# A decoder layer's MLP with its activation tiles 32 bytes lower in SBUF

## The chip, the cores and the metric

The kernel runs on one core of a Trainium2 chip. The metric is the device time of one execution in microseconds (us); 1 us is 1000 ns. A "matmul" below is one matmul instruction of TensorE: it streams a **moving** operand (up to 512 columns, one result column each) past a **stationary** operand (128 columns), which a weight load (LDWEIGHTS, engine name PEld in the profile) has put into the array before.

## The reference

One layer of a hybrid decoder on 512 tokens of width 1024, in float32. The change lies in the last part, the MLP:

```python
h = h + mixed @ w_o[l]
a = jax.nn.relu(rmsnorm(h, g_mlp_norm[l]) @ w_up[l])   # (512, 4096)
h = h + (a * a) @ w_down[l]                            # (512, 1024)
...
return rmsnorm(h, g_final)
```

## The kernel before

**Split products.** Every float32 operand is split into a high and a low part (`split`, L121), and a product is three matmuls, `mm3` (L129): high times high, high times low, low times high, into one PSUM bank. In the profile L130, L131 and L132 are these three.

**The MLP.** The 4096 hidden columns are done in four quarters (L1132). A quarter first computes two units of up-projection (`up_unit`, L1005; the first of all is `up_plain`, L1044), 512 hidden columns each, and then two halves of down-projection (L1141), 512 output columns each. The up-projection's matmuls (L991) have 256 columns: the stationary operand is a 128-column slice of a weight tile `uw`, the moving operand 256 columns of a token tile `tt...`. The down-projection's matmuls (`down`, L1148) have 512 columns: the stationary operand is a 128-column slice of the activations, `ah` (high part) or `al` (low part), and the moving operand is half a row of a tile `dw` of W_down. In the last half of the last quarter the fourth token block is done in pieces of 256 columns (`pieces`, L1127). TensorE does its matmuls in program order; the loads, splits and additions for later tiles run on the other engines beside them.

**Where the tiles lie.** A tile's address is the same in all 128 partitions, and pools are laid behind each other in the order in which they are opened:

- The pool `nsa` holds the five slots (`slot`, L934) in which the weight tiles `uw` and `dw` lie. A slot has 2048 or 2176 columns of 4 bytes: 16 or 17 times 512 bytes. The pool's other tiles are multiples of 512 bytes too.
- Then comes the pool `mh` (L925): a tile `shift` of 8 columns (32 bytes) that nothing reads, then the seven tiles `tt` of 8192 bytes, and raw weights and sums of 4096 bytes each.
- Then comes the pool `mlp` (L1094): a tile `back` of 120 columns (480 bytes) that nothing reads, then `gf` (4096 bytes, the final gain), seven tiles `c` of 2048 bytes (snapshots, `re`, `v`, `jh`, `jf`, `fin`), and eight tiles `ah` and eight `al` of 2048 bytes.

All slices that the matmuls take start at multiples of 128 columns, which is 512 bytes. So, counted in multiples of 512 bytes, `ah` and `al` lie at the same place as `uw` and `dw` (32 + 480 = 512), and `tt` lies 32 bytes above it.

Of the kernel before, what the change touches and what calls it, by code (L numbers as in the profile page):

```python
# [10 lines left out]
F32 = mybir.dt.float32  # L11
# [6 lines left out]
P = 128  # L18
# [76 lines left out]
def layer(ctx, tc, x, xt, w_in, w_uq, w_ukv, w1k, w2k, w1v, w2v, w_o, w_up, w_down, g_final, consts, vecs, out):  # L95
# [997 lines left out]
    m["wo"].release()  # L1093
    mp = ctx.enter_context(tc.tile_pool(name="mlp", **reuse))  # L1094

    mp.tile([P, 120], F32, name="back")
    gf = mp.tile([P, D], F32, name="gf")
    sync.dma_start(gf, g_final.unsqueeze(0).to_broadcast([P, D]))
    fs, rf, fin = col(80, 16), col(40), {}
# [162 lines left out]
```

## Time and profile before

| | |
|---|---|
| median of 3 runs | 648.17 us (647.2 to 648.53) |
| the profiled execution | 648.08 us |
| its span, first to last instruction | 646.2 us |
| TensorE matmuls busy | 628.8 us (97%) |
| mean granted TensorE clock | 0.999 |

The span is what the rows show; the 1.9 us between it and the execution's time lie around it. Start times in the rows count from the start of the span. A matmul's own duration contains its way through the array; what the next one has to wait is the step from one start to the next, which is read from the start times.

### The profile page before, as it was taken

What the parts mean: (1) busy time and instruction counts of PE and PEld (TensorE: products, weight loads), DVE (VectorE), ACT (ScalarE), POOL (GpSimd) and SP (SyncE); (2) the same over time, 40 slices, a digit from 0 to 9 for tenths busy, and PEclk for the clock granted to TensorE, in tenths of its full rate; (3) what the DMA queues carried; (4) which work ended last, traced back from release to release, by engine and by line L of the source; (5) the groups of instructions that cost most, each with busy time, mean ns of one, the idle gap of its engine ahead of it and who ended that gap; (6) DMA issues with size and microseconds to landing.
All of it is one profiled execution on the core that took longest, in us unless ns stands there. A gap on an engine that the chain in (4) does not pass through costs nothing.

```text
span 646.2 us, 10981 instructions
## 1 busy us (share of the span) xinstructions
PE 628.8 (97%) x4092; PEld 568.1 (88%) x4092; DVE 430.4 (67%) x898; ACT 337.2 (52%) x702; POOL 243.2 (38%) x294
## 2 busy tenths in 40 slices
PE   7989999999999999999999999999999999999996
PEld 5989999998878888888998889988899888999885
DVE  5767577756778598869967436784259843497425
ACT  5567677867946487741794115451144521355213
POOL 3764402235783138713111325413155231354031
PEclk9999999999999999999999999999999999999999
DMA  6533210105323101063035313254121542124003
GB/s 192 161 92 87 69 43 25 33 2 183 97 83 101 32 2 34 2 194 133 33 101 166 126 33 99 70 183 139 33 73 63 183 139 67 64 68 146 17 2 130
DMA packets 47125, 56.53 MB, mean 87 GB/s; under 512 B 4320, under 2 KB 34784, under 8 KB 47072
## 3 DMA queue, kind: packets, MB, share of 16 engines
q1 hardware_dynamic: 46784, 55.57, 27.5%
q8 instruction: 32, 0.52, 0.3%
q10 hardware_dynamic: 288, 0.26, 0.1%
q14 instruction: 21, 0.17, 0.1%
HBM read 53.72 MB, written 2.10 MB: 86 GB/s over the span
## 4 chain that ended last, share of the span: by engine, by line
PE 86%; DVE 5%; DMA 3%; ACT 2%; POOL 2%; issue 1%; SPq 1%; POOLq 0%; ACTq 0%; DVEq 0%
PE up_ps L991 25%; PE dn_ps L131 9%; PE dn_ps L132 9%; PE dn_ps L130 9%; PE wo_ps L132 2%; PE wo_ps L130 2%; PE wo_ps L131 2%; PE pt_ps L585 2%; PE hid_ps L730 2%; PE pt_ps L692 1%; PE s_ps L547 1%; PE ot_ps L596 1%; PE wq_ps L131 1%; PE wq_ps L132 1%; PE wq_ps L130 1%
## 5 line engine op out<-in xcount | busy, mean ns | idle before, releaser
L130 PE MATMUL dn_ps<-dw,ah 128*128 128x512 f32 (+1 forms) x264 | 101.1, 383 | 0.0
L131 PE MATMUL dn_ps<-dw,ah 128*128 128x512 f32 (+1 forms) x264 | 101.1, 383 | 0.0
L132 PE MATMUL dn_ps<-dw,al 128*128 128x512 f32 (+1 forms) x264 | 100.8, 383 | 0.0
L991 PE MATMUL up_ps<-ttT,uw 128*128 128x256 f32 x720 | 87.8, 279 | 1.9 <-ACT snap L1020 1.9
L991 PEld LDWEIGHTS up_ps<-ttT,uw 128*128 128x128 f32 x720 | 85.6, 188 | 2.5 <-ACT snap L1020 2.5
L991 PE MATMUL up_ps<-ttB,uw 128*128 128x256 f32 x648 | 80.4, 279 | 0.0
L991 PEld LDWEIGHTS up_ps<-ttB,uw 128*128 128x128 f32 x648 | 78.1, 188 | 0.5
L959 POOL TENSOR_TENSOR us<-us,ur 128x1024 f32<-128x1024 f32 x14 | 41.7, 2978 | 96.3 <-DVE uw L125 96.3
L959 POOL TENSOR_TENSOR us<-ur 128x1024 f32<-128x1024 f32 x14 | 35.0, 2511 | 98.3 <-DMA ur<-in_w_up 49.2
L125 DVE TENSOR_TENSOR dw<-dr,dw 128x1024 fp32r<-128x1024 f32 x32 | 44.0, 1374 | 33.5 <-ACT dw L111 33.5
L125 DVE TENSOR_TENSOR uw<-us,uw 128x1024 fp32r<-128x1024 f32 x28 | 34.2, 1223 | 45.6 <-ACT uw L111 45.6
L131 PEld LDWEIGHTS dn_ps<-dw,ah 128*128 128x128 f32 x264 | 49.6, 188 | 9.7
L130 PEld LDWEIGHTS dn_ps<-dw,ah 128*128 128x128 f32 x264 | 49.6, 188 | 9.7
L132 PEld LDWEIGHTS dn_ps<-dw,al 128*128 128x128 f32 x264 | 49.5, 188 | 9.6
L111 ACT CAST uw<-us 128x1024 fp32r<-128x1024 f32 x28 | 29.4, 1051 | 54.3 <-PE dn_ps L132 39.7
L125 DVE TENSOR_TENSOR uw<-ur,uw 128x1024 fp32r<-128x1024 f32 x25 | 40.1, 1605 | 25.0 <-ACT uw L111 25.0
L111 ACT CAST dw<-dr 128x1024 fp32r<-128x1024 f32 x32 | 33.3, 1050 | 36.2 <-PE dn_ps L132 20.8
L111 ACT CAST uw<-ur 128x1024 fp32r<-128x1024 f32 x25 | 26.3, 1051 | 28.7 <-PE dn_ps L132 26.2
L125 DVE TENSOR_TENSOR pl<-pt_ps,ph 128x512 fp32r<-128x512 f32 (+3 forms) x60 | 34.3, 578 | 8.2 <-ACT ph L111 7.0
L560 ACT ACTIVATE pr<-pr,mx 128x256 f32<-128x256 f32 (+3 forms) x64 | 36.0, 565 | 6.5 <-DVE mx L552 4.6
L111 ACT CAST ph<-pt_ps 128x512 fp32r<-128x512 f32 (+3 forms) x60 | 29.7, 499 | 15.6 <-PE pt_ps L585 5.4
L1158 DVE SCALAR_TENSOR_TENSOR xs<-dn_ps,small,xs 128x512 f32<-128x512 f32 (+1 forms) x33 | 22.8, 734 | 19.0 <-PE dn_ps L132 19.0
(326 smaller groups left out, 1540.5 us busy)
## 6 DMA issues: line engine op xcount, KB each, us to landing
ur<-in_w_up SPq DMA_DIRECT2D x32, 512.0 KB, 3.8
dr<-in_w_down SPq DMA_DIRECT2D x32, 512.0 KB, 3.7
wor<-in_w_o SPq DMA_DIRECT2D x16, 256.0 KB, 3.0
wqraw<-in_w_in SPq DMA_DIRECT2D x16, 128.0 KB, 2.2
xs<-in_x SPq DMA_DIRECT2D x4, 512.0 KB, 5.1
wmraw<-in_w_in SPq DMA_DIRECT2D x8, 208.0 KB, 4.5
xr<-in_xt SPq DMA_DIRECT2D x3, 512.0 KB, 3.6
out<-xs SPq DMA_DIRECT2D x6, 256.0 KB, 2.2
```

What stands on the lines that cost most here:

```text
L111: nc.scalar.copy(dst, src)
L125: (lo_eng or nc.vector).tensor_tensor(lo, src, hi.bitcast(F32), op=ALU.subtract)
L130: nc.tensor.matmul(o, a_hi, b_hi, start=first, stop=False)
L131: nc.tensor.matmul(o, a_hi, b_lo, start=False, stop=False)
L132: nc.tensor.matmul(o, a_lo, b_hi, start=False, stop=last)
L547: nc.tensor.matmul(S[:, :b - a], qs, ka[:, brg, a:b], start=True, stop=False)
L560: nc.scalar.activation(pr[:, :L], pr[:, :L], AF.Exp, bias=lim, scale=-1.0, accum_out=sums[:, 4 + h:5 + h])
L585: nc.tensor.transpose(b[:, h * P:(h + 1) * P], prs[h][:, j * P:(j + 1) * P], ident)
L730: nc.tensor.matmul(hp[0:96, 0:P], xx[:, 2 * i:2 * i + 16 * 95 + 1:16], w1[:, j, :], start=(i == 0), stop=(i == 15))
L959: add = lambda o, x, y: nc.gpsimd.tensor_tensor(o, x, y, op=ALU.add)
L991: nc.tensor.matmul(oj, v[:, x, k, s], t[:, y, k, :], start=first and j == 0 and k == 0 and n == 0, stop=k == 3 and n == 2, skip_group_chec ...
L1158: nc.vector.scalar_tensor_tensor(xs[:, t, cs], accs[t, a][:, a:b], r4[:, t:t + 1], xs[:, t, cs], op0=ALU.mult, op1=ALU.add)
```

## The change

The unread tile `back` shrinks from 120 to 112 columns, from 480 to 448 bytes. Everything in the pool `mlp`, `gf`, `c`, `ah` and `al`, then lies 32 bytes lower. No instruction is added, removed or moved to another place in its queue. `uw`, `dw` and `tt` stay where they are. Counted in multiples of 512 bytes, `dw` then lies 32 bytes above `ah` and `al`.

```diff
-    mp.tile([P, 120], F32, name="back")
+    mp.tile([P, 112], F32, name="back")
     gf = mp.tile([P, D], F32, name="gf")
```

## Rows read from the trace of the kernel before

**Rows 1.** The profile page: span, busy time of TensorE, granted TensorE clock in tenths over 40 slices, and the shares of the chain that ended last.

```profile
span 646.2 us, 10981 instructions
...
PE 628.8 (97%) x4092; PEld 568.1 (88%) x4092; DVE 430.4 (67%) x898; ACT 337.2 (52%) x702; POOL 243.2 (38%) x294
...
PEclk9999999999999999999999999999999999999999
...
PE 86%; DVE 5%; DMA 3%; ACT 2%; POOL 2%; issue 1%; SPq 1%; POOLq 0%; ACTq 0%; DVEq 0%
```

**Rows 2.** Matmuls by line and shape from 344.7 to 640 us (four quarters but the first up-projection): count, busy us, mean ns of one, idle us before them.

```profile
L131 PE MATMUL dn_ps<-dw,ah 128*128 128x512 f32 x248 | 96.6, 389 | 0.0
L130 PE MATMUL dn_ps<-dw,ah 128*128 128x512 f32 x248 | 96.6, 389 | 0.0
L132 PE MATMUL dn_ps<-dw,al 128*128 128x512 f32 x248 | 96.5, 389 | 0.0
L991 PE MATMUL up_ps<-ttT,uw 128*128 128x256 f32 x577 | 70.8, 279 | 1.9 <-ACT snap L1020 1.9
L991 PE MATMUL up_ps<-ttB,uw 128*128 128x256 f32 x432 | 53.9, 279 | 0.0
L132 PE MATMUL dn_ps<-dw,al 128*128 128x256 f32 x16 | 4.5, 282 | 0.0
L131 PE MATMUL dn_ps<-dw,ah 128*128 128x256 f32 x16 | 4.5, 282 | 0.0
L130 PE MATMUL dn_ps<-dw,ah 128*128 128x256 f32 x16 | 4.5, 281 | 0.0
```

**Rows 3.** Busy time of each engine, with its count of instructions, the granted clock and the DMA share, in an up-projection unit (388 to 408 us) and in the two halves of the down-projection that follow the next one.

```profile
388.00:408.00 20.00, 20.00 (x173) 19.96 (x172) 13.75 (x12) 9.92 (x12) 11.90 (x5) 1.00 0.27 84
...
428.30:450.00 21.70, 21.70 (x98) 17.98 (x97) 12.71 (x16) 5.87 (x7) 5.00 (x2) 1.00 0.50 158
450.00:471.90 21.90, 21.90 (x99) 18.12 (x98) 7.83 (x9) 4.20 (x4) 4.79 (x2) 1.00 0.13 41
```

**Rows 4.** The second quarter's down-projection: its first matmul, the first one of the up-projection behind it, and (by line, 428.4 to 471.8 us) the count of one of its three lines.

```profile
428.32 0.39 PE L130 MATMUL dn_ps<-dw,ah 128*128 128x512 f32 x1
...
471.85 0.86 PE L991 MATMUL up_ps<-ttB,uw 128*128 128x256 f32 x6
...
L131 PE MATMUL dn_ps<-dw,ah 128*128 128x512 f32 x64 | 24.9, 389 | 0.0
```

**Rows 5.** The last pieces of the down-projection, 256 columns each: the first two and the last of 23 matmuls that follow each other without another instruction of TensorE between them.

```profile
636.89 0.28 PE L131 MATMUL dn_ps<-dw,ah 128*128 128x256 f32 x1
637.01 0.28 PE L132 MATMUL dn_ps<-dw,al 128*128 128x256 f32 x1
...
639.53 0.28 PE L132 MATMUL dn_ps<-dw,al 128*128 128x256 f32 x1
```

**Rows 6.** The instructions in order of time: start us, duration us. A matmul of the down-projection and the weight load for the next one.

```profile
615.90 0.39 PE L132 MATMUL dn_ps<-dw,al 128*128 128x512 f32 x1
615.91 0.19 PEld L130 LDWEIGHTS dn_ps<-dw,ah 128*128 128x128 f32 x1
```

**Rows 7.** The chain that ended last, in order of time: start us, length us, line and count of the matmuls. Three stretches of up-projection without a wait.

```profile
307.87 36.87 PE up_ps L991 x316
388.31 33.62 PE up_ps L991 x288
...
472.01 33.62 PE up_ps L991 x288
```

**Rows 8.** Two projections at the start of the kernel: the first and the last of 31 matmuls of `wm_ps` (416 columns) and of 24 matmuls of `wk_ps` (256 columns), each without another instruction of TensorE between them.

```profile
21.39 0.34 PE L130 MATMUL wm_ps<-wmh,xth 128*128 128x416 f32 x1
...
27.06 0.36 PE L130 MATMUL wm_ps<-wmh,xth 128*128 128x416 f32 x1
...
43.13 0.28 PE L130 MATMUL wk_ps<-wkh,xth 128*128 128x256 f32 x1
...
45.85 0.28 PE L132 MATMUL wk_ps<-wkh,xtl 128*128 128x256 f32 x1
```

**Rows 9.** ScalarE copies of 128 by 512 from PSUM, to a tile of the pool `mlp` and to tiles of two other pools: count, busy us, mean ns.

```profile
L1020 ACT COPY snap<-up_ps 128x512 f32<-128x512 f32 x21 | 12.3, 583 | 12.0 <-PE up_ps L991 12.0
L637 ACT COPY os<-ot_ps 128x512 f32<-128x512 f32 x16 | 9.3, 584 | 8.4 <-PE ot_ps L597 6.1 <-PE ot_ps L704 2.3
L590 ACT COPY pb<-pt_ps 128x512 f32<-128x512 f32 x12 | 7.0, 582 | 1.7 <-PE pt_ps L585 1.7
```

**Rows 10.** An up-projection behind a wait of 0.64 us: its last 45 matmuls in two merged rows; the down-projection begins at 428.32 us [rows 4].

```profile
422.91 3.10 PE L991 MATMUL up_ps<-ttT,uw 128*128 128x256 f32 x24 [0.64 <-ACT snap L1020]
425.84 2.63 PE L991 MATMUL up_ps<-ttB,uw 128*128 128x256 f32 x21
```

**Rows 11.** The first quarter's down-projection: its first matmul and the eleventh.

```profile
344.57 0.40 PE L130 MATMUL dn_ps<-dw,ah 128*128 128x512 f32 x1
...
346.89 0.39 PE L131 MATMUL dn_ps<-dw,ah 128*128 128x512 f32 x1
```

## The prediction, made before the changed kernel ran

> **What bounds the kernel now.** I read the page first. TensorE is busy for 97% of the span, at the upper of its two clock levels (2.4 GHz) in every slice, and holds 86% of the chain that ended last [rows 1]. So the time is the sum of TensorE's steps, and only what changes such a step, or opens a gap between two, can move it. Next I read the matmuls by line and shape: from 344.7 us on, the down-projection is 744 matmuls of 512 columns and 48 of 256, 792 in all, with no idle time before any of them; the only idle time is 1.9 us in the up-projection, waiting for a snapshot on ScalarE [rows 2]. The table of stretches shows how much room the others have: in the down-projection's two halves TensorE is busy throughout, while VectorE works 12.7 and 7.8 us of 21.8, ScalarE 5.9 and 4.2 [rows 3]. The reader is to see that nobody else sets the pace there.
>
> Last I read the steps from start to start, since the 389 ns that a row gives for a 512-column matmul contain its way through the array. The second quarter's down-projection takes 471.85 - 428.32 = 43.53 us for 3 x 64 = 192 matmuls: **226.7 ns** each [rows 4]. Its small pieces of 256 columns take (639.53 - 636.89) / 22 = **120.0 ns** [rows 5]. 256 more columns cost 106.7 ns, so a column costs 0.417 ns (one at each beat of 2.4 GHz), and both shapes carry the same extra: 226.7 - 213.3 = 120.0 - 106.7 = **13.3 ns** a matmul, whatever its length.
>
> **Where the 13.3 ns may come from.** The weight load for the next matmul starts 0.01 us behind the start of the present one and lasts 0.19 us [rows 6]: two streams read SBUF side by side, the moving operand and the next stationary one. If they get into each other's way, it matters how their addresses stand to each other, and it costs per weight load, not per column, as the 13.3 ns do. The kernel has the test built in. The up-projection has the same three-matmul pattern, 256 columns and 128 stationary columns, but its moving tile `tt` lies 32 bytes above the stationary `uw`, modulo 512. It steps by 36.87/316 = 116.7, 33.62/288 = 116.7 and again 116.7 ns [rows 7]. Same shape, other distance: 116.7 against 120.0. The extra is **10.0 ns** at 32 bytes against 13.3 at zero, 3.3 less. The means of one say the same, 279 against 282 ns [rows 2].
>
> Two other stages fit. The `wm` projection's tiles are 416 columns, 13 times 128 bytes, so its distances are multiples of 128 bytes; it steps by (27.06 - 21.39)/30 = 189.0 ns, and 416 columns at 0.417 are 173.3: an extra of 15.7. The `wk` projection's tiles are 280 columns (35 times 32 bytes), so its distance changes with every tile through all multiples of 32; it steps by (45.85 - 43.13)/23 = 118.3, an extra of 11.6, between the two [rows 8]. So a distance that stays at zero (modulo 128) is the dear end, a mixture lies between, and a steady 32 bytes is the cheap end of what the trace shows.
>
> **The change part by part.** (1) `ah` and `al` move down 32 bytes, `dw` stays: the moving operand then lies 32 bytes above the stationary one, with the sign and the size that the up-projection has now. The trace has no 512-column matmul at that distance. From the cheap side the nearest row is the up-projection's 10.0 ns [rows 7], from the dear side no gain, 13.3 [rows 4], or even `wm`'s 15.7 [rows 8]. I take 10.0: the extra did not depend on the length at distance zero, so I let it not depend on it at 32 bytes, and order and lines of the three matmuls are the same. The sum: 792 x 3.33 ns = **2.64 us** less. A 512-column step would be 223.3 ns, a half of the down-projection 96 x 223.3 = 21.44 us instead of 21.76.
>
> (2) `gf` and the `c` tiles move too. Their users are ScalarE, VectorE and GpSimd. ScalarE's 128 by 512 copy takes 583 ns into a `c` tile and 584 and 582 ns into tiles of two other pools that lie elsewhere [rows 9], so I cost the shift at nothing. What hides it is TensorE's unbroken stream [rows 2]; without that cover 2 ns on the 21 snapshots would be 0.04 us.
>
> (3) Is anything late when the down-projection is 0.32 us shorter per half? What must be ready by then are the next weight tiles. ScalarE and VectorE rest for at least 9 us in each half [rows 3], and no matmul there waits [rows 2]. The three waits of 0.64 us for a snapshot [rows 10] lie inside an up-projection and are timed from its own matmuls; they stay.
>
> The Trainium skill speaks against this change. Its page "TensorE: Matmul & The Clock Gate", section "Step-by-step: what each phase is for", gives TensorE two independent read ports of SBUF and says that loading the next weights takes no read bandwidth from the running matmul; its section "Back-to-back issue gap" puts the step at N/2.4 + 2.5 ns, an estimate of 109.2 ns for 256 columns. The trace disagrees: the same shape steps by 120.0 and 116.7 ns [rows 5, 7]. By that page the change would do nothing.
>
> **Rivals.**
>
> *Half the gain.* TensorE can settle into more than one rhythm at the same distance. Behind the wait, the up-projection's 21 matmuls take 428.32 - 425.84 = 2.48 us, 118.1 ns each [rows 4, 10], an extra of 11.4, and it stays so up to the down-projection. Today the rhythm re-forms there, as the distance changes; with equal distances it might be carried over. `wk`'s mixture has about the same extra, 11.6 [rows 8]. Gain (13.3 - 11.4) x 792 = 1.5 us: 646.6 us.
>
> *No change.* The 3.3 ns belong to something else that differs between the up- and the down-projection: where the moving operand itself lies (`tt` against `dw`, and `dw` does not move), or 512 columns hide what 256 do not. For it: in the rows of one stage the distance never varies alone. Against it: 13.3 at both lengths [rows 4, 5]. Time 648.1. This is also where the skill's two ports end.
>
> *Slower.* The two streams meet later instead of less. At the first matmuls of the first quarter's down-projection the step is (346.89 - 344.57)/10 = 232 ns [rows 11], an extra of 18.7, before it settles at 13.3: a stream of 512 columns can be held in a dearer rhythm. If 32 bytes keep it from settling, the price runs from `wm`'s 15.7, 2.4 x 792 = 1.9 us, to 5.4 x 792 = 4.3 us: 650.0 to 652.4 us. It decides as soon as the 512-column step is over 226.7 ns. Against it: the up-projection's long stretches settle at the same distance [rows 7].
>
> **How the numbers follow.** The full gain has 0.53: 648.08 - 2.64 = 645.44 us. The profiled execution lies 0.09 us under the median of the runs, so 645.5 is forecast for the median. Half the gain has 0.13, no change 0.22, slower 0.12. The runs before spread over 1.3 us, 0.2% of the time, so 0.2% (1.3 us) is about what can be told from no change. Of half the gain, at 1.5 us, I count two thirds as faster and the rest as the same: faster 0.53 + 0.09 = 0.62, same 0.22 + 0.04 = 0.26, slower 0.12. The range reaches from the full gain less what a run spreads downward (645.5 - 1.0 = 644.5) to no change with its spread upward and a small part of the slower case (648.8); outside it lie most of the slower case and little below.
>
> **What would show it.** Right: steps of 223 to 224 ns in the second quarter's down-projection, 42.9 us for its 192 matmuls, mean of one near 386 ns, pieces of 256 columns at 117 ns, up-projection unchanged at 116.7 ns, and still only three waits. Half: 224.8 ns. Wrong: 226.7 as before with the total unmoved, which would put the 3.3 ns on the moving tile's own place or on the length; or steps over 226.7. The prediction would also fail in part if the down-projection gains and the up-projection, entered in another rhythm, goes from 116.7 to 118.1 ns: seven units of 7 products of 24 matmuls, 1176 times 1.4 ns, give 1.6 us back.

## The result, and the profile after

The changed kernel is slower: a median of 652.07 us (651.81 to 653.21) against 647.68 us for four runs of the kernel before, a ratio of **1.0064, 95% interval 1.0048 to 1.0081**. 645.5 us had been forecast, with a range of 644.5 to 648.8.

The page of the kernel after, with the lines that answer to [rows 1]:

```profile
span 651.3 us, 10981 instructions
...
PE 634.8 (97%) x4092; PEld 568.9 (87%) x4092; DVE 430.9 (66%) x898; ACT 337.3 (52%) x702; POOL 243.3 (37%) x294
...
PEclk9999999999999999999999999999999999999999
...
PE 84%; DVE 6%; DMA 3%; ACT 2%; issue 2%; POOL 1%; SPq 1%; POOLq 0%; ACTq 0%; DVEq 0%
```

TensorE bounds it as before, at the same clock level. The span is 5.1 us longer and TensorE's busy time 6.0 us; the weight loads' (PEld) 0.8 us longer, and every other engine's is within 0.5 us.

Matmuls by line and shape from 344.7 to 650 us, answering to [rows 2]:

```profile
L131 PE MATMUL dn_ps<-dw,ah 128*128 128x512 f32 x248 | 98.0, 395 | 0.0
...
L991 PE MATMUL up_ps<-ttT,uw 128*128 128x256 f32 x583 | 71.4, 279 | 1.9 <-ACT snap L1020 1.9
...
L131 PE MATMUL dn_ps<-dw,ah 128*128 128x256 f32 x16 | 4.5, 280 | 0.0
L130 PE MATMUL dn_ps<-dw,ah 128*128 128x256 f32 x16 | 4.5, 280 | 0.0
L132 PE MATMUL dn_ps<-dw,al 128*128 128x256 f32 x16 | 4.5, 279 | 0.0
```

Two opposite things have happened. The down-projection's 256-column pieces went from 282 to 280 ns, as forecast; its 512-column matmuls went from 389 to 395 ns, against the forecast. The up-projection and its 1.9 us of waits stayed. The start times say it more sharply (timeline of TensorE, to set beside [rows 4] and [rows 5]):

```profile
430.20 0.39 PE L130 MATMUL dn_ps<-dw,ah 128*128 128x512 f32 x1
...
474.99 0.40 PE L991 MATMUL up_ps<-ttB,uw 128*128 128x256 f32 x2
...
642.13 0.28 PE L131 MATMUL dn_ps<-dw,ah 128*128 128x256 f32 x1
...
644.70 0.28 PE L132 MATMUL dn_ps<-dw,al 128*128 128x256 f32 x1
```

The second quarter's 192 matmuls take 44.79 us, **233.3 ns** a step instead of 226.7; 22 steps of the pieces take 2.57 us, **116.8 ns** instead of 120.0. With a column at 0.417 ns, the extra at 32 bytes is 20.0 ns for 512 columns and 10.1 for 256. And the up-projection, in the chain that ended last, as in [rows 7]:

```profile
308.54 36.86 PE up_ps L991 x316
390.19 33.62 PE up_ps L991 x288
...
475.15 33.62 PE up_ps L991 x288
```

116.6 and 116.7 ns as before. So the whole difference lies in the 744 long matmuls: 744 x 6.6 = 4.9 us more, 48 x 3.2 = 0.2 us less, about 4.7 us together; the medians differ by 4.4 us. The two spans differ by more, 5.1 us, because the profiled execution of the changed kernel was 0.7 us late before any matmul had read a moved tile: the first of these stretches starts at 308.54 us, against 307.87.

### The profile page after: what moved, and what is told of

It reads as the page before. It is cut to its first block, busy times and chain, and to the rows that moved or that the text cites. A ratio compares the mean times of both kernels' runs of the same rounds, so it can differ in the third digit from the quotient of the medians.

```text
span 651.3 us, 10981 instructions
## 1 busy us (share of the span) xinstructions
PE 634.8 (97%) x4092; PEld 568.9 (87%) x4092; DVE 430.9 (66%) x898; ACT 337.3 (52%) x702; POOL 243.3 (37%) x294
## 4 chain that ended last, share of the span: by engine, by line
PE 84%; DVE 6%; DMA 3%; ACT 2%; issue 2%; POOL 1%; SPq 1%; POOLq 0%; ACTq 0%; DVEq 0%
PE up_ps L991 24%; PE dn_ps L131 9%; PE dn_ps L132 9%; PE dn_ps L130 9%; PE wo_ps L130 2%; PE wo_ps L132 2%; PE wo_ps L131 2%; PE pt_ps L585 2%; PE hid_ps L730 2%; PE s_ps L547 1%; PE ot_ps L596 1%; PE wq_ps L130 1%; PE pt_ps L692 1%; PE wq_ps L131 1%; PE wq_ps L132 1%
## 5 line engine op out<-in xcount | busy, mean ns | idle before, releaser
L130 PE MATMUL dn_ps<-dw,ah 128*128 128x512 f32 (+1 forms) x264 | 102.4, 388 | 0.0
L131 PE MATMUL dn_ps<-dw,ah 128*128 128x512 f32 (+1 forms) x264 | 102.4, 388 | 0.0
L132 PE MATMUL dn_ps<-dw,al 128*128 128x512 f32 (+1 forms) x264 | 102.2, 388 | 0.0
L991 PE MATMUL up_ps<-ttT,uw 128*128 128x256 f32 x720 | 87.7, 279 | 1.9 <-ACT snap L1020 1.9
L991 PEld LDWEIGHTS up_ps<-ttT,uw 128*128 128x128 f32 x720 | 85.5, 188 | 2.5 <-ACT snap L1020 2.5
L991 PE MATMUL up_ps<-ttB,uw 128*128 128x256 f32 x648 | 80.4, 279 | 0.0
L991 PEld LDWEIGHTS up_ps<-ttB,uw 128*128 128x128 f32 x648 | 78.1, 188 | 0.5
L131 PEld LDWEIGHTS dn_ps<-dw,ah 128*128 128x128 f32 x264 | 49.5, 187 | 11.3
L130 PEld LDWEIGHTS dn_ps<-dw,ah 128*128 128x128 f32 x264 | 49.5, 187 | 11.2
L132 PEld LDWEIGHTS dn_ps<-dw,al 128*128 128x128 f32 x264 | 49.4, 187 | 11.3
L1158 DVE SCALAR_TENSOR_TENSOR xs<-dn_ps,small,xs 128x512 f32<-128x512 f32 (+1 forms) x33 | 23.2, 734 | 20.2 <-PE dn_ps L132 20.2
```

What stands on the lines that cost most here:

```text
L130: nc.tensor.matmul(o, a_hi, b_hi, start=first, stop=False)
L131: nc.tensor.matmul(o, a_hi, b_lo, start=False, stop=False)
L132: nc.tensor.matmul(o, a_lo, b_hi, start=False, stop=last)
L991: nc.tensor.matmul(oj, v[:, x, k, s], t[:, y, k, :], start=first and j == 0 and k == 0 and n == 0, stop=k == 3 and n == 2, skip_group_chec ...
L1158: nc.vector.scalar_tensor_tensor(xs[:, t, cs], accs[t, a][:, a:b], r4[:, t:t + 1], xs[:, t, cs], op0=ALU.mult, op1=ALU.add)
```

## The experiments

Steps are read from start times as above. "Extra" is the step less 0.417 ns for each moving column; "distance" is moving minus stationary address, modulo 512. The whole times of `acts_low`, `rest_low`, `both_down`, `dw_up`, `al_low`, `up_192` and `dist_c` are to be set beside 648.42 us, the median of the kernel before in the runs beside them; their ratios are to that. The diffs show only the lines in question, and line numbers shift by a few with an edit (L991 is L992 or L994 in some kernels).

**Which part of the change costs the time.** `acts_low` moves only `ah` and `al`, `rest_low` only `gf` and the `c` tiles.

```diff
# acts_low, in activated(); back stays at 120 columns
+        if "pad" not in m:
+            m["pad"] = mp.tile([P, 120], F32, name="pad")
         ah = mp.tile([P, T], R32, tag="ah", name="ah", bufs=8)
# rest_low, the same place; back has 112 columns
+            m["pad"] = mp.tile([P, 8], F32, name="pad")
```

> One part of the change alone: ah and al lie 32 bytes lower modulo 512 (an unread tile of 480 bytes just ahead of them), gf and the c tiles stay. Theory 'distance': all of the change's cost is here, 233.3 ns a step in the down-projection and 652.1 us. Rival 'other operands' (ScalarE, VectorE and GpSimd on the shifted c tiles and gf cost part of it): less than 652.

> The other part alone: gf and the c tiles lie 32 bytes lower, ah and al where they were (an unread tile of 32 bytes between). Theory 'distance': as before, 226.7 ns a step, 648 us. Rival 'other operands': slower than before.

Measured: `acts_low` 653.1 us, ratio to the kernel before 1.0069 (1.0054 to 1.0084); `rest_low` 647.87 us, 0.9992 (0.9983 to 1.0002). The second quarter's down-projection of `acts_low`, first matmul and the one behind the last:

```profile
430.26 0.40 PE L130 MATMUL dn_ps<-dw,ah 128*128 128x512 f32 x1
...
475.06 0.40 PE L991 MATMUL up_ps<-ttB,uw 128*128 128x256 f32 x2
```

and of `rest_low`:

```profile
428.03 0.40 PE L130 MATMUL dn_ps<-dw,ah 128*128 128x512 f32 x1
...
471.59 0.28 PE L991 MATMUL up_ps<-ttB,uw 128*128 128x256 f32 x1
```

44.80 us, 233.3 ns a step, against 43.56 us, 226.9. All of the cost is in where `ah` and `al` lie; the operands of the other engines play no part that can be measured.

**The distance, or a tile's own place.** `both_down` puts an unread tile of 480 bytes, `dw_up` one of 32 bytes, ahead of everything in the pool of the weight slots.

```diff
+    nsa.tile([P, 120], F32, name="lead")   # both_down; back stays at 120
+    nsa.tile([P, 8], F32, name="lead")     # dw_up; back 112
     ka = ring("k", "ka", (4, 32 + T))
```

> An unread tile of 480 bytes ahead of the weight slots moves uw, dw, tt, ah and al together; counted modulo 512 all of them lie 32 bytes lower than before, so ah and al lie where the change puts them, but the distances are those of the kernel before (0 in the down-projection, 32 in the up-projection). Theory 'distance': steps as before, 226.7 and 116.7 ns. Theory 'place of the stationary tile': as changed, 233.3 ns in the down-projection.

> The changed kernel with an unread tile of 32 bytes ahead of the weight slots: ah and al lie, modulo 512, where they lay before the change, and uw, dw and tt lie 32 bytes higher; distance 32 in both projections. Theory 'distance': 233.3 ns in the down-projection, 116.7 in the up-projection. Theory 'place of the stationary tile': 226.7 ns. (Theory 'place of the moving tile' would give a change here that neither the changed kernel nor both_down shows.)

Measured, in one run each: 647.25 us and 652.69 us. The second quarter's down-projection of `both_down`:

```profile
427.44 0.39 PE L130 MATMUL dn_ps<-dw,ah 128*128 128x512 f32 x1
...
471.00 0.86 PE L992 MATMUL up_ps<-ttB,uw 128*128 128x256 f32 x6
```

and of `dw_up`:

```profile
429.67 0.39 PE L130 MATMUL dn_ps<-dw,ah 128*128 128x512 f32 x1
...
474.45 1.80 PE L992 MATMUL up_ps<-ttB,uw 128*128 128x256 f32 x14
```

43.56 us, 226.9 ns, and 44.78 us, 233.2 ns. With `ah` and `al` where the change puts them the step is the old one as long as `dw` has moved along, and with `ah` and `al` at their old place it is the new one as soon as `dw` has moved away. It is the distance that counts, not where either tile lies.

**The length.** `len_32` is the changed kernel and `len_0` the kernel before, with shorter moving or narrower stationary operands in three quarters of the matmuls of six of the eight halves. They leave the rest of each product out, so only their steps are used and not their whole times (639.62 and 638.53 us).

```diff
+    MN = ((128, 512), (128, 448), (128, 384), (128, 320), (96, 512), (64, 512), (32, 512), (128, 512))
-                s = slice(256 * j + 128 * (t % 2), 256 * j + 128 * (t % 2) + 128)
+                full = (n, j) in ((0, 0), (3, 1))
+                w, b = (128, b) if full or last else (MN[2 * quarter + c][0], MN[2 * quarter + c][1])
+                s = slice(256 * j + 128 * (t % 2), 256 * j + 128 * (t % 2) + w)
-                mm3(accs[t, a][:, a:b], ...
+                mm3(accs[t, a][:w, a:b], ...
```

> The changed kernel (distance +32), but in each half of the down-projection the six middle ones of eight groups of matmuls do only a part: halves 1 to 7 have 512, 448, 384, 320 moving columns with 128 stationary ones, then 512 moving with 96, 64 and 32 stationary columns; the rest of the product is left out. Theory 'per column': at +32 the extra grows with the moving columns, 10.0 ns per 256: steps of 233.3, 204.2, 175.0, 145.8 ns. Theory 'two levels': the extra is 20.0 ns for whatever is over 256 columns: 233.3, 206.7, 180.0, 153.3. Both of them with the extra coming from the weight load beside the matmul: with 96, 64, 32 stationary columns the extra falls to about 15, 10, 5 ns (228, 223, 218). If the moving operand alone makes it, 233.3 stays for all three.

> The kernel before (distance 0) with the same parts left out as in len_32. Extra fixed at 13.3 ns at every length: steps of 226.7, 200.0, 173.3, 146.7 ns. If it comes from the weight load beside the matmul, one stall for so many stationary columns: 96, 64, 32 give an extra of 10, 6.7, 3.3 ns: 223.3, 220.0, 216.7. If not: 226.7 for all three.

The timeline of `len_32`: the first of 72 matmuls of 448, 384 and 320 columns and the matmul behind the last; then the first and the last of 71 matmuls with 96 and of 72 with 32 stationary columns:

```profile
369.75 0.37 PE L130 MATMUL dn_ps<-dw,ah 128*128 128x448 f32 x1
...
384.63 0.40 PE L130 MATMUL dn_ps<-dw,ah 128*128 128x512 f32 x1
...
430.36 0.34 PE L130 MATMUL dn_ps<-dw,ah 128*128 128x384 f32 x1
...
443.08 0.40 PE L130 MATMUL dn_ps<-dw,ah 128*128 128x512 f32 x1
...
448.68 0.31 PE L130 MATMUL dn_ps<-dw,ah 128*128 128x320 f32 x1
...
459.24 0.39 PE L130 MATMUL dn_ps<-dw,ah 128*128 128x512 f32 x1
...
504.96 0.39 PE L130 MATMUL dn_ps<-dw,ah 128*96 128x512 f32 x1
...
520.82 0.39 PE L131 MATMUL dn_ps<-dw,ah 128*96 128x512 f32 x1
...
589.25 0.40 PE L130 MATMUL dn_ps<-dw,ah 128*32 128x512 f32 x1
...
605.83 0.40 PE L132 MATMUL dn_ps<-dw,al 128*32 128x512 f32 x1
```

And of `len_0`, the first of 72 matmuls of 320 columns and the matmul behind the last:

```profile
448.11 0.30 PE L130 MATMUL dn_ps<-dw,ah 128*128 128x320 f32 x1
...
458.67 0.39 PE L130 MATMUL dn_ps<-dw,ah 128*128 128x512 f32 x1
```

Worked out from such rows of both kernels (step, and the extra in brackets, ns; the 256-column values are the pieces', the full 512-column values those of the kernels before and after):

```
moving x stationary    distance 0       distance 32
256 x 128              120.0 (13.3)     116.8 (10.1)
320 x 128              146.7 (13.3)     146.7 (13.3)
384 x 128              173.8 (13.8)     176.7 (16.7)
448 x 128              202.6 (16.0)     206.7 (20.0)
512 x 128              226.7 (13.3)     233.3 (20.0)
512 x 96               229.9 (16.5)     226.6 (13.2)
512 x 64               230.0 (16.7)     230.9 (17.5)
512 x 32               231.7 (18.4)     233.5 (20.2)
```

At distance zero the length matters little, only 448 stands out. At 32 bytes the extra grows with the length, 3.3 ns for every 64 columns up to 448. Neither theory's line fits: "per column" gave 145.8, 175.0 and 204.2 for 320, 384 and 448, "two levels" 153.3, 180.0 and 206.7. At 320 columns the two distances are equal, and of the lengths measured only 256 is better off at 32 bytes. The extra doesn't fall in step with the stationary columns: at zero it rises from 13.3 to 18.4 ns as they go from 128 to 32, and at 32 bytes it drops from 20.0 to 13.2 at 96 columns and is back at 20.2 at 32. So it is no stall that each loaded column causes.

**The curve over the distance.** Three kernels put `ah` and `al` side by side into a wider tile and place them anew in each quarter. `dist_a` and `dist_b` also move the seven `tt` tiles one by one. The room comes from one buffer of raw weights, and these kernels are slower as wholes (665.29, 658.05 and 660.12 us): in `dist_a` TensorE waits 6.5 us in the up-projection instead of 1.9, and its mean granted clock in the stretch behind one of these waits (428 to 432.5 us) is 0.62, so part of it runs at the lower level. Only their settled steps at the upper level are used. The edits of `tt`, `back` and the buffer are not shown.

```diff
-        ah = mp.tile([P, T], R32, tag="ah", name="ah", bufs=8)
-        al = mp.tile([P, T], R32, tag="al", name="al", bufs=8)
+        hl = mp.tile([P, 2 * T + 128], R32, tag="ah", name="ah", bufs=8)
+        o = OFF[quarter]       # dist_a: 120, 8, 112, 96 columns; _b: 64, 104, 124, 16; _c: 88, 4, 2, 116
+        ah, al = hl[:, o:o + T], hl[:, o + T:o + 2 * T]
```

> The step from start to start is read by stage. The distance is moving minus stationary, modulo 512. Down-projection, 512 columns: quarter 1 at +32, quarter 2 at -32, quarter 3 at +64, quarter 4 at +128 bytes (dw stays, ah and al move inside a wider tile). Up-projection, 256 columns: 0 for B11, 32 for T1, 64 for B21, 96 for T3, 128 for T2, 256 for T4, 384 for B22 (uw stays, tt moves). One buffer fewer for raw weights makes room, so waits may appear between the stretches. Theory 'distance': the distance alone sets the step, so +32 gives 233.3 ns in the down-projection and the up-projection 120.0 at 0 and 116.7 at 32; at 64 and 128 anything between 216 and 236 ns, and -32 need not be like +32. Theory 'place': it is where the moved tile itself lies, modulo 64, that counts: ah at an even multiple of 32 from its old place (64, 128) gives 226.7, at an odd one (+32, -32) 233.3; up 120.0 at 0, 64, 128, 256, 384 and 116.7 at 32, 96. Theory 'rhythm': distance plays no part and the step is a matter of what came before; then the four quarters agree within 1 ns.

> As dist_a with other distances. Down-projection: quarter 1 at 256, quarter 2 at 96, quarter 3 at 16, quarter 4 at -64 bytes. Up-projection: 160 for B11, 192 for T1, 224 for B21, 288 for T3, 320 for T2, 448 for T4, 480 for B22. Theory 'distance': one curve through both kernels, the up- and the down-projection each on its own; if it repeats every 128 bytes, 256 in the down-projection gives 226.7 like 0. Theory 'place': 256, -64 give 226.7, 96 gives 233.3, 16 something else; up 120.0 at 192, 320, 448 and 116.7 at 160, 224, 288, 480. Theory 'rhythm': all quarters within 1 ns.

> As dist_a (wider tiles, one buffer fewer for raw weights) with all of the up-projection at 192 bytes and the down-projection at 160, -16, -8 and 48 bytes in quarters 1 to 4. Theory 'distance': another four points of the curve for 512 columns; between 0 (226.7), 16 (228.3) and 32 (233.3) it rises, so 48 lies between 32's 233.3 and 64's 228.9, and -8 and -16 between 226.7 and 233.3. If a point falls below 226.7 it is a better place for the down-projection. Up-projection: 115.1 ns in all products.

The third quarter of `dist_a` (64 bytes), its first matmul and the one behind its 192nd:

```profile
524.07 0.39 PE L130 MATMUL dn_ps<-dw,ah 128*128 128x512 f32 x1
...
568.03 0.40 PE L994 MATMUL up_ps<-ttB,uw 128*128 128x256 f32 x2
```

The first and the third quarter of `dist_b` (256 and 16 bytes):

```profile
344.81 0.39 PE L130 MATMUL dn_ps<-dw,ah 128*128 128x512 f32 x1
...
388.35 0.40 PE L994 MATMUL up_ps<-ttB,uw 128*128 128x256 f32 x2
...
518.44 0.40 PE L130 MATMUL dn_ps<-dw,ah 128*128 128x512 f32 x1
...
562.29 0.29 PE L994 MATMUL up_ps<-ttB,uw 128*128 128x256 f32 x1
```

43.96, 43.54 and 43.85 us for 192 matmuls: 229.0, 226.8 and 228.4 ns. All points of the curve, mean steps of the settled matmuls in ns (the up-projection's distances change with every product, after 24 or 48 matmuls):

```
512 columns   0: 226.7   16: 228.3   32: 233.3   48: 232-233   64: 228.9   96: 233.3   128: 232.5
              160: 234.3   256: 226.7   -64: 233.4   -32: 233.3   -16: 233.3   -8: 230.7
256 columns   0: 119.4   32: 118.0   64: 117.8   96: 119.6   128: 118.8   160: 118.0   192: 115.1
              224: 118.2   256: 119.4   288: 116.9   320: 117.9   384: 118.6   448: 115.8   480: 118.2
```

"Rhythm" alone (all quarters alike) falls, and so does "place modulo 64": 64, 128 and -64 would give 226.7. In the down-projection 256 is like 0; in the up-projection the values 256 apart agree within 0.8 ns but for 32 and 288 (1.1). For 512 columns zero and 256 are the lowest points measured, and nine of the other eleven are dearer by 4 to 8 ns; for 256 columns zero is among the dearest. The order is not reversed as a whole: 96 is dear at both lengths.

Some of the values for 256 columns are means over more than one pace. A product at 32 bytes reads 118.0 here, between products at other distances, and 116.7 in [rows 7], where a whole up-projection lies at 32; and 115.1 at 192 is a mean of stretches at 113.3 and at 117.8 ns. `dist_c`, whose up-projection lies at 192 bytes throughout, shows the two apart, and not the 115.1 that was expected of it: 168 matmuls of the second quarter, then 168 of the third, each from its first to the one behind its last.

```profile
391.13 0.39 PE L994 MATMUL up_ps<-ttT,uw 128*128 128x256 f32 x2
...
410.17 0.50 PE L994 MATMUL up_ps<-ttT,uw 128*128 128x256 f32 x3
...
478.77 0.40 PE L994 MATMUL up_ps<-ttT,uw 128*128 128x256 f32 x2
...
498.56 0.52 PE L994 MATMUL up_ps<-ttT,uw 128*128 128x256 f32 x3
```

19.04 us, 113.3 ns, and 19.79 us, 117.8 ns. The one follows a down-projection at 160 bytes, the other one at -16: at the same distance there are two paces, and what ran before is the likely reason.

**Two distances in turn.** `al_low` lowers `al` alone by 32 bytes.

```diff
+        if "pad" not in m:
+            m["pad"] = mp.tile([P, 120], F32, name="pad")
         al = mp.tile([P, T], R32, tag="al", name="al", bufs=8)
```

> The kernel before with al alone 32 bytes lower: distance 0 where the stationary tile is ah, 32 where it is al. al's weight load runs beside the second matmul of a triple (L131), al is the own stationary tile of the third (L132). If the load beside the matmul sets its step: L131 233.3, the other two 226.7 ns. If the matmul's own stationary tile sets it: L132 233.3. In both cases a mean of 228.9 ns. If the step follows from a rhythm over several matmuls, the three don't separate so, and the mean may lie anywhere between 226.7 and 235 ns.

Measured: 650.96 us in one run. The first quarter's 192 matmuls:

```profile
344.18 0.40 PE L130 MATMUL dn_ps<-dw,ah 128*128 128x512 f32 x1
...
388.55 0.40 PE L991 MATMUL up_ps<-ttB,uw 128*128 128x256 f32 x2
```

44.37 us, 231.1 ns a step and not 228.9. By line the steps from start to start are 226.8, 235.0 and 231.6 ns (L130, L131, L132) in the first quarter and 233.1, 231.3 and 232.1 in the second: the same addresses, another pattern. So neither the load beside a matmul nor its own stationary tile sets its step by itself; the step belongs to a rhythm over several matmuls, into which TensorE settles differently from quarter to quarter.

**A better place for the up-projection.** `up_192` follows the curve's lowest point for 256 columns.

```diff
-    mh.tile([P, 8], F32, name="shift")
+    mh.tile([P, 48], F32, name="shift")
-    mp.tile([P, 120], F32, name="back")
+    mp.tile([P, 80], F32, name="back")
```

> The kernel before with tt 192 instead of 32 bytes above uw (shift of 48 columns, back of 80, so the down-projection stays at distance 0). Theory 'distance': dist_b's 115.1 ns at 192 for one product in seven holds for all, against 116.8 now: 1368 matmuls x 1.7 ns = 2.3 us less, 645.4 us; the down-projection stays at 226.7 ns. Theory 'rhythm of the neighbours' (115.1 was due to the products around it): the step stays at 116.7 and the time at 647.7 us.

Measured: 647.33 us, ratio **0.9981 (0.9972 to 0.9990)**: faster than both kernels, but by 1.1 us and not by the 2.3 expected. Its chain that ended last:

```profile
307.61 35.83 PE up_ps L991 x316
...
386.97 33.93 PE up_ps L991 x288
421.66 5.39 PE up_ps L991 x45
```

113.4 ns in the first stretch, 117.8 in the second, at one and the same distance: behind its down-projection at distance zero it settles into a dearer rhythm than the 116.7 ns of [rows 7]. The first up-projection gives 1.0 us (316 x 3.3 ns). The later long stretches lose 0.3 us each (33.93 against 33.62) and get most of that back right behind them: the wait for the snapshot, timed from their own matmuls, falls from 0.64 to 0.42 us, 1.3 us for the three instead of 1.9. So nearly the whole gain is the first up-projection's.

## Why the prediction was wrong

**What bounds the kernel: right.** TensorE's steps made the time before and after, and no wait was added or removed (1.9 us in both).

**That the distance between the two operands moves the step: right**, and shown by `both_down`, `dw_up`, `acts_low` and `rest_low`. That it alone sets the step is not: `dist_c` and `up_192` have two paces at one distance for 256 columns. The rival of no change, with the moving tile's own place as its reason, is out. The Trainium skill's rule behind that rival ("TensorE: Matmul & The Clock Gate", "Step-by-step: what each phase is for": two independent read ports) and its sentence "PE and ACT never wait on anyone" ("SBUF — State Buffer", "Who interferes with whom") disagree with these runs as far as one takes them to mean that addresses don't matter: moving the stationary tile alone by 32 bytes took the step from 226.7 to 233.3 ns.

**The shift of the other tiles at nothing: right** (`rest_low` 0.9992).

**The 256-column pieces at 117 ns: right** (116.8), and the up-projection unchanged: right.

**The 512-column step at 223.3 ns: wrong, and this step decided.** It stood in part (1) of the change: "the extra did not depend on the length at distance zero, so I let it not depend on it at 32 bytes". It does at 32 bytes: 10.1, 13.3, 16.7, 20.0 and 20.0 ns at 256, 320, 384, 448 and 512 columns (`len_32`). The term was to be 744 x -3.3 = -2.5 us and is 744 x +6.6 = +4.9 us. The evidence for it was one distance at two lengths and one length at two distances; the fourth corner, which the change needed, was the one that the trace did not have, and the two factors don't add.

**What the rows had said against it.** The prediction read `wm`'s extra of 15.7 at 416 columns [rows 8] as the dear end of distance zero. Its distances were multiples of 128, and 128 costs 512 columns 232.5 ns in `dist_a`, where zero costs 226.7: distances don't count modulo 128, and the row spoke of length and distance together. The slower rival had the direction and its price, 650.0 to 652.4 us for "a stream of 512 columns held in a dearer rhythm", and 652.07 lies in it, though the extra (20.0) is above the highest row used for it (18.7, [rows 11]). Its argument against, that the up-projection settles at the same distance, was an argument about 256 columns. The measured difference, 4.4 us, is likewise just above its upper end of 4.3; 652.07 is inside because the kernel before ran 0.5 us faster in these runs than in those of the forecast. The chance of 0.12 was too low for a case whose only counter-argument came from the other length.

**The Trainium skill's step** for 256 columns, 109.2 ns as an estimate from "TensorE: Matmul & The Clock Gate", section "Back-to-back issue gap", is given there for a matmul by itself and not, as the prediction has it, for a stream of weight loads and matmuls like this one. No run here came down to it: the lowest settled stretches are at 113.3 and 113.4 ns (`dist_c` and `up_192`).

## What to carry to other kernels

Where a kernel lives on back-to-back matmuls with a new weight load for each, the distance between the addresses of the moving and the stationary operand is worth a look. Here it was worth some 3% of a 512-column step, and as far as measured it counted modulo 256 bytes. It must be measured at the very length in question: 192 bytes had the lowest steps for 256 columns, and the point that is like it modulo 256, -64 bytes, cost 512 columns 233.4 ns. Read steps from start to start, take several hundred of them, and look whether a stretch is in one rhythm or in two before a mean is carried over to another stage. A price read at two corners of a square (one shape, one distance each) says nothing safe of the fourth corner.

## What the runs showed of the hardware

That one and the same stream has more than one steady pace was known from the trace before; that the paces lie so far apart was not: 113.4 and 117.8 ns at 192 bytes with 256 columns. With fewer stationary columns the extra does not fall at distance zero: 13.3, 16.5, 16.7 and 18.4 ns for 128, 96, 64 and 32 of them. What makes the distance count is not settled: that the weight load beside the matmul is the other party is likely, since `ah` and `al`, the only operands of TensorE that the change moves, are read by it, but no run shows how the two reads get into each other's way, nor why the length matters at 32 bytes and not at zero.
